# Weight sums in buffers of their own, and activation factors split one stage earlier

## The chip, the core and the metric

The kernel runs on one core of one Trainium2 chip. The metric is the device time of one execution in microseconds. The core has a matrix engine (TensorE, PE in the profile; PEld is its weight load), a vector engine (VectorE, DVE), a scalar engine (ScalarE, ACT), GpSimd (POOL) and SyncE (SP), which here only issues DMAs. Each engine takes its instructions in the order in which they stand in its queue: one that waits holds up all behind it.

## What is computed

One residual layer over 512 tokens of width 2048, then the final norm:

```python
h = rmsnorm(x, norm1_g)
u = h @ cc_w_in + cc_b_in
val, gate = jnp.split(u, 2, axis=-1)
u = causal_dwconv(val * jax.nn.sigmoid(gate), cc_dw) + cc_dw_b
x = x + (jax.nn.silu(layernorm(u, cc_ln_g, cc_ln_b)) @ cc_w_out + cc_b_out)
h2 = rmsnorm(x, norm2_g)
x = x + jnp.square(jax.nn.relu(h2 @ mlp_w1)) @ mlp_w2
out = rmsnorm(x, final_g)
```

`mlp_w1` is 2048 x 8192, `mlp_w2` is 8192 x 2048. All is float32.

## The kernel before

Every float32 matrix product is made of three products of a shorter type, fp32r: each factor is rounded to a high part (`wh`, `ah`) and the rest is its low part (`wl`, `al`), and `mm3` (L277) adds high x high, high x low and low x high. The profile shows them as L280, L281 and L282.

The first half of the program is the convolution layer. This case is about the MLP behind it, in two stages.

**The first product** (L790 to L840) runs over 64 tiles f of 128 hidden units. For each, two chunks of weights are loaded, split (`Plain.make`, L121: high part on ACT, low part on DVE or POOL) and multiplied with the 16 tiles of h2. DVE takes the result out with relu and a scale (L823), ACT squares it (L824). Two f make a pair n. The result of a pair is a 2 x 2 block matrix of 256 tokens by 128 hidden units: a11, a12, a21, a22, and POOL makes four sums of it (s1 to s4, L832 to L835). Seven left factors of 256 columns, a11, a22, a12 and the four sums, are written to DRAM (`spill[n]`) by DMAs that ACT issues, one for the three blocks and one for the four sums.

**The second product** uses a scheme of seven products for a 2 x 2 block product: P1 to P7, each of one left factor (sum of activation blocks) and one right factor (a block or difference of blocks of `mlp_w2`). It runs over 8 groups g of four pairs. A group has two passes q (the two halves of the output columns); a pass (`seven`, L848) has 14 chunks, the seven products for each half hs of the group, in the order ORDER. I write P5,1 for product P5 of half 1. A chunk is 12 matmuls with one pair of `wh` and `wl`: two pairs i of the half, two halves of 128 tokens, three matmuls each. In the last group, only half 0 is done this way, and the last two pairs are multiplied plainly (`last_pair`, L896).

The right factors are made by `Factor.make` (L151). `Sums.get` (L135) loads the four blocks b11, b12, b21, b22 of a half, in one buffer each. POOL makes the differences, each written over one of its own inputs: P5 = b12 - b11 into b11 (L162), P6 into b11 (L165), P7 into b12 (L168), P4 into b11 (L171). ACT rounds the factor to `wh` (L172), ACT copies `wh` to the matrix engine's accumulators (`ax`, L178) and DVE subtracts (L179, two halves of a chunk); for P2 alone POOL subtracts (L174).

**Buffers.** The ring of `wh` has four buffers, so has that of `wl`: a chunk's high part is made when the chunk four before has been used. Blocks b12 and b22 lie in the four "raw" buffers that also carry the plain weights, b11 and b21 in five "rb" buffers, which in the first product hold `four` and `sums`.

**Activation factors.** `fetch(n)` (L774) loads the seven factors of a pair as they are into one of two buffers `seven`, by a DMA of SP; `prepare(n)` (L779) rounds and subtracts them on ACT (L786) and DVE (L787) into `ah` and `al` of one of seven slots. The tables FETCH and PREP say behind which chunk (q, step) of a group this is put for the four pairs of the next group. A slot is free when the pair seven before has been used.

Outside the stretches marked as scheduled by hand, a scheduler sets the order of each engine's instructions when the program is built.

Of the kernel before, what the change touches and what calls it, by code (L numbers as in the profile page):

```python
# [57 lines left out]
BLOCKS = ("11", "12", "21", "22")  # L58
# [21 lines left out]
HT = T // 2  # L80
# [3 lines left out]
def trunk(ctx: ExitStack, tc: tile.TileContext, xT, vec, fg, w_in, w_out, w1, w2s, w2b, out):  # L84
    nc = tc.nc
# [7 lines left out]
    wts = ctx.enter_context(tc.tile_pool(name="wts", bufs=4))  # L93
# [7 lines left out]
    dram = ctx.enter_context(tc.tile_pool(name="dram", bufs=1, space=bass.MemoryType.DRAM))  # L101
# [26 lines left out]
    class Sums:  # L128


        def __init__(self, src):
            self.src = src
            self.raw = {}

        def get(self, b, hs):  # L135
            if (b, hs) not in self.raw:
                pool, tag, n = (wts, "raw", 4) if b[1] == "2" else (mlp[0], "rb", 5)
                t = pool.tile([P, 1024], F32, tag=tag, name=f"b{b}", bufs=n)
                nc.sync.dma_start(out=t, in_=self.src[BLOCKS.index(b), hs])
                self.raw[b, hs] = t  # L140
            return self.raw[b, hs]

    class Factor:
# [5 lines left out]
                self.sums.get(b, self.hs)  # L149

        def make(self, hi, lo):  # L151
            b11, b12, b21, b22 = (self.sums.raw.get((b, self.hs)) for b in BLOCKS)
            sub = ALU.subtract
            if self.product == "P1":
                s = b11
            elif self.product == "P2":
                s = b21
            elif self.product == "P3":
                s = b22
            elif self.product == "P5":  # L160
                s = b11
                nc.gpsimd.tensor_tensor(out=s, in0=b12, in1=b11, op=sub)  # L162
            elif self.product == "P6":
                s = b11
                nc.gpsimd.tensor_tensor(out=s, in0=b22, in1=b11, op=sub)  # L165
            elif self.product == "P7":
                s = b12
                nc.gpsimd.tensor_tensor(out=s, in0=b22, in1=b12, op=sub)  # L168
# [3 lines left out]
            nc.scalar.copy(out=hi, in_=s)  # L172
            if self.product in LO_POOL:
                nc.gpsimd.tensor_tensor(out=lo, in0=s, in1=hi.bitcast(F32), op=sub)  # L174
                return
            for sl in (slice(0, 512), slice(512, 1024)):
                st = bank("ax")
                nc.scalar.copy(out=st, in_=hi[:, sl].bitcast(F32))  # L178
                nc.vector.tensor_tensor(out=lo[:, sl], in0=s[:, sl], in1=st, op=sub)  # L179
# [585 lines left out]

    NPAIR = FF // P // 2
    LASTS = NPAIR - GROUP // 4
    spill = [dram.tile([P, 7 * HT], F32, name=f"spill{n}") for n in range(NPAIR)]
    acc = []
    row2 = None  # L770
    pairs = {}
    raws = {}

    def fetch(n):  # L774
        raws[n] = mlp[0].tile([P, 7 * HT], F32, tag="seven", name="seven", bufs=2)
        width = 7 * HT if n < LASTS else 4 * HT
        nc.sync.dma_start(out=raws[n][:, :width], in_=spill[n][:, :width])

    def prepare(n):  # L779

        seven = raws.pop(n)
        i = n % SLOTS
        hi = slots[i].tile([P, 7 * HT], F32R, tag=f"ah{i}", name="ah", bufs=1)
        lo = slots[i].tile([P, 7 * HT], F32R, tag=f"al{i}", name="al", bufs=1)
        for sl in (slice(0, 3 * HT), slice(3 * HT, 7 * HT)):
            nc.scalar.copy(out=hi[:, sl], in_=seven[:, sl])  # L786
            nc.vector.tensor_tensor(out=lo[:, sl], in0=seven[:, sl], in1=hi[:, sl].bitcast(F32), op=ALU.subtract)  # L787
        pairs[n] = (hi, lo)

    for f in range(FF // P):  # L790
        ps = bank()
        for c in range(2):
            wh, wl = chunk()
            for i in range(8):
                k = 8 * c + i
                sl = slice(i * P, (i + 1) * P)
                mm3(ps, (wh[:, sl], wl[:, sl]), h2[k], k == 0, k == NT - 1)
        if row2 is None:
            st = bank("ax")
            col_sums(st, acc1)  # L800
# [24 lines left out]
        if n >= LASTS:
            nc.scalar.dma_start(out=spill[n][:, f % 2 * T :][:, :T], in_=here)
        elif f % 2:
            a21, a11, a22, a12 = (four[:, i * HT : (i + 1) * HT] for i in range(4))
            sums = mlp[0].tile([P, 4 * HT], F32, tag="rb", name="sums", bufs=5)
# [5 lines left out]
            nc.gpsimd.tensor_tensor(out=s4, in0=a12, in1=s2, op=ALU.subtract)  # L835
            nc.scalar.dma_start(out=spill[n][:, 3 * HT :], in_=sums)
        if f >= FF // P - 8 and f % 2 == 0 and f < FF // P - 2:
            fetch((f - (FF // P - 8)) // 2)
        elif f >= FF // P - 8 and f % 2 and f < FF // P - 2:
            prepare((f - (FF // P - 7)) // 2)  # L840
# [4 lines left out]
    prepare(3)  # L845


    def seven(g, q, halves):  # L848
# [20 lines left out]
        for step, (product, hs) in enumerate(ORDER):  # L869
# [36 lines left out]

    for q in range(2):
# [18 lines left out]
    for b in range(NTOK):  # L926
# [6 lines left out]
        for i, cs in enumerate(pieces):  # L933
# [9 lines left out]
            sq = mlp[0].tile([P, 1024], F32, tag="rb", name="sq", bufs=5)  # L943
# [61 lines left out]
```

## Time and profile before

| | us |
|---|---|
| three runs | 1999.8, 1999.65, 1997.3 (median 1999.65) |
| profiled execution, device time | 1997.83 |
| its span, first to last instruction | 1996.0 |
| mean granted TensorE clock over the span | 0.987 |
| first product, about | 600 to 1288 |
| second product | 1288 to 1945 |
| norm and output behind it | 1945 to 1996 |

The page divides the span into 40 slices; slices 13 to 25 are the first product, 26 to 39 the second. "idle before us <-releaser" in a row of the profile is the time the engine stood still ahead of such an instruction, and who ended the wait.

```profile
PE   6999999989999999999999999998989889898998
DVE  8999999971142311111111111377676766777675
ACT  5443444462343322222222222377676666776662
POOL 5799899746642433333333333465455565555563
```

In the first product (1 to 4 tenths on DVE, ACT and POOL) the other engines have much room; in the second DVE and ACT are at 6 to 7 tenths, and PE has slices of 8.

### The profile page before, as it was taken

To read this page: it belongs to the slowest core of one execution; us is meant where nothing else is said; L and a number is where in the kernel's file an instruction comes from. 1 tells how busy PE (TensorE), PEld (TensorE's weight loads), DVE (VectorE), ACT (ScalarE), POOL (GpSimd) and SP (SyncE) were. 2 spreads that over 40 slices of the span, in tenths; PEclk is the share of its full clock that TensorE was granted. 3 is DMA by queue.
4 is the path that set the end of the run, shared out by engine and by line. 5 is a ranking of instruction groups with operands and counts; after the bars stand their busy time and mean duration, and the time that the engine had idled before them with its cause. 6 is when DMAs were issued, how large, how long until landed. Compare 5 with 4: busy or idle time off the path is not lost.

```text
span 1996.0 us, 23068 instructions
## 1 busy us (share of the span) xinstructions
PE 1908.2 (96%) x8578; PEld 1567.2 (79%) x8578; DVE 1082.8 (54%) x1512; ACT 923.3 (46%) x1286; POOL 1084.5 (54%) x625
## 2 busy tenths in 40 slices
PE   6999999989999999999999999998989889898998
PEld 4888888988888888888888888877777777777776
DVE  8999999971142311111111111377676766777675
ACT  5443444462343322222222222377676666776662
POOL 5799899746642433333333333465455565555563
PEclk9999999999999999999999999999999999999999
DMA  5222332133234444334343433344443433343323
GB/s 215 87 85 95 107 136 95 33 127 121 91 106 144 174 158 150 134 132 150 132 141 138 147 132 137 133 165 132 164 148 127 158 118 125 121 157 131 116 85 106
DMA packets 73552, 257.15 MB, mean 129 GB/s; under 512 B 8160, under 2 KB 8800, under 8 KB 73440
## 3 DMA queue, kind: packets, MB, share of 16 engines
q1 hardware_dynamic: 63792, 225.99, 33.5%
q10 hardware_dynamic: 9648, 29.69, 3.7%
q8 instruction: 67, 1.10, 0.2%
q14 instruction: 45, 0.37, 0.1%
HBM read 222.88 MB, written 32.77 MB: 128 GB/s over the span
## 4 chain that ended last, share of the span: by engine, by line
PE 58%; DVE 14%; issue 12%; POOL 10%; DMA 3%; ACT 1%; SPq 0%; POOLq 0%; DVEq 0%; ACTq 0%
PE mm L281 17%; PE mm L282 16%; PE mm L280 16%; PE mm L651 8%; DVE ax L356 4%; POOL b L162 4%; POOL b L168 3%; DMA b<-in_w2s 3%; DVE wl L179 2%; DVE x L866 2%; POOL wl L174 2%; POOL b L171 1%; DVE al L787 1%; POOL b L165 1%; DVE xl L274 1%
## 5 line engine op out<-in xcount | busy, mean ns | idle before, releaser
L126 POOL TENSOR_TENSOR wl<-raw,wh 128x1024 fp32r<-128x1024 f32 x151 | 365.3, 2430 | 508.6 <-ACT wh L125 505.8
L125 ACT CAST wh<-raw 128x1024 fp32r<-128x1024 f32 (+1 forms) x221 | 230.1, 1048 | 631.4 <-PE mm L281 399.0
L281 PE MATMUL mm<-yl,wh 128*128 128x512 f32 x1024 | 398.7, 389 | 0.2 <-DVE yl L274 0.2
L280 PE MATMUL mm<-yh,wh 128*128 128x512 f32 x1024 | 398.7, 389 | 0.0
L282 PE MATMUL mm<-yh,wl 128*128 128x512 f32 x1024 | 398.6, 389 | 0.0
L281 PE MATMUL mm<-wl,ah 128*128 128x512 f32 x840 | 339.3, 404 | 36.7 <-DVE wl L179 24.9
L280 PE MATMUL mm<-wh,ah 128*128 128x512 f32 x840 | 331.2, 397 | 16.2 <-ACT wh L172 14.3
L282 PE MATMUL mm<-wh,al 128*128 128x512 f32 x840 | 332.9, 397 | 0.0
L179 DVE TENSOR_TENSOR wl<-b,ax 128x512 fp32r<-128x512 f32 x360 | 231.5, 681 | 169.0 <-ACT ax L178 92.6
L172 ACT CAST wh<-b 128x1024 fp32r<-128x1024 f32 x210 | 217.2, 1050 | 191.9 <-POOL b L162 127.1
L126 DVE TENSOR_TENSOR wl<-raw,wh 128x1024 fp32r<-128x1024 f32 (+1 forms) x70 | 89.5, 1279 | 353.8 <-ACT wh L125 353.8
L281 PEld LDWEIGHTS mm<-wl,ah 128*128 128x128 f32 x840 | 161.5, 192 | 87.7 <-DVE wl L179 35.4
L281 PEld LDWEIGHTS mm<-yl,wh 128*128 128x128 f32 x1024 | 192.2, 188 | 40.3 <-DVE yl L274 0.6
L280 PEld LDWEIGHTS mm<-yh,wh 128*128 128x128 f32 x1024 | 192.2, 188 | 39.8
L282 PEld LDWEIGHTS mm<-yh,wl 128*128 128x128 f32 x1024 | 192.2, 188 | 39.7
L356 DVE SCALAR_TENSOR_TENSOR ax<-u,v,ax 128x512 f32<-128x512 f32 x327 | 218.2, 751 | 0.0
L280 PE MATMUL mm<-xh,wh 128*128 128x512 f32 (+1 forms) x544 | 206.4, 379 | 5.5 <-ACT wh L125 5.4
L282 PE MATMUL mm<-xh,wl 128*128 128x512 f32 (+1 forms) x544 | 205.9, 379 | 4.0 <-DVE wl L126 4.0
L281 PE MATMUL mm<-xl,wh 128*128 128x512 f32 (+1 forms) x544 | 206.9, 380 | 2.5 <-DVE xl L274 2.4
L178 ACT COPY ax<-wh 128x512 f32<-128x512 f32 x360 | 200.6, 585 | 17.7 <-DVE wl L179 15.1
L280 PEld LDWEIGHTS mm<-wh,ah 128*128 128x128 f32 x840 | 160.5, 192 | 55.9 <-ACT wh L172 17.8
L162 POOL TENSOR_TENSOR b<-b,b 128x1024 f32<-128x1024 f32 x30 | 77.2, 2574 | 222.6 <-DVE wl L179 209.8
(172 smaller groups left out, 2577.5 us busy)
## 6 DMA issues: line engine op xcount, KB each, us to landing
raw<-in_w SPq DMA_DIRECT2D x128, 512.0 KB, 3.3
b<-in_w2s SPq DMA_DIRECT2D x120, 512.0 KB, 4.3
raw<-in_w_in SPq DMA_DIRECT2D x63, 512.0 KB, 3.3
seven<-spill SPq DMA_DIRECT2D x30, 896.0 KB, 4.7
raw<-in_w_out SPq DMA_DIRECT2D x32, 512.0 KB, 3.3
spill<-sums ACTq DMA_DIRECT2D x30, 512.0 KB, 2.6
spill<-four ACTq DMA_DIRECT2D x30, 384.0 KB, 2.3
xt<-in_xT SPq DMA_DIRECT2D x16, 256.0 KB, 5.8
```

The source lines that it names most:

```text
L125: nc.scalar.copy(out=hi[:, sl], in_=raw[:, sl])
L126: (nc.vector if sl.stop == cut else self.eng).tensor_tensor(out=lo[:, sl], in0=raw[:, sl], in1=hi[:, sl].bitcast(F32), op=ALU.subtract)
L162: nc.gpsimd.tensor_tensor(out=s, in0=b12, in1=b11, op=sub)
L168: nc.gpsimd.tensor_tensor(out=s, in0=b22, in1=b12, op=sub)
L172: nc.scalar.copy(out=hi, in_=s)
L178: nc.scalar.copy(out=st, in_=hi[:, sl].bitcast(F32))
L179: nc.vector.tensor_tensor(out=lo[:, sl], in0=s[:, sl], in1=st, op=sub)
L280: nc.tensor.matmul(out=ps, lhsT=wh, rhs=xh, start=first, stop=False, **how)
L281: nc.tensor.matmul(out=ps, lhsT=wh, rhs=xl, start=False, stop=False, **how)
L282: nc.tensor.matmul(out=ps, lhsT=wl, rhs=xh, start=False, stop=last, **how)
L356: nc.vector.scalar_tensor_tensor(out=o, in0=a, scalar=w, in1=c, op0=ALU.mult, op1=ALU.add)
L651: nc.tensor.matmul(out=ps[n][:, sl], lhsT=a[:, wsl], rhs=x[:, sl], start=first and a is wh and x is hi, stop=last and x is lo)
```

## The change

- P5's difference gets a buffer of its own, b5, in the "raw" ring, next to b22. P6 = b22 - b5 is written over b11, P7 over b12 as before, P4 = b21 - b11 over b21. So b11, b12 and b21 lie in "rb", which has eight buffers instead of five: twelve buffers for ten blocks and differences of a pass instead of nine for eight. Blocks are asked for three items ahead instead of two.
- The activation factors are rounded and split in the first product's stage (`split`), and both parts are written to DRAM: four DMAs per pair instead of two, with twice the bytes. The DMA of a low part is issued behind the next tile's square (the list `later`). `prepare`, its instructions in the second product and the buffers `seven` are gone.
- `fetch` loads high and low part straight into the slot, by two DMAs of GpSimd; FETCH has new places, and the first three pairs are fetched behind tiles 8, 10 and 12 of the first product. `last_pair` fetches in the same way.

```diff
-PREP = ((0, 3), (0, 9), (1, 2), (1, 12))
-FETCH = ((0, 0), (0, 4), (0, 10), (1, 3))
+FETCH = ((0, 2), (0, 6), (0, 10), (1, 12))
...
+        def buffer(self, b):
+
+            pool, tag, n = (wts, "raw", 4) if b in ("22", "5") else (mlp[0], "rb", 8)
+            return pool.tile([P, 1024], F32, tag=tag, name=f"b{b}", bufs=n)
...
             elif self.product == "P5":
-                s = b11
-                nc.gpsimd.tensor_tensor(out=s, in0=b12, in1=b11, op=sub)
+                raw["5", hs] = self.sums.buffer("5")
+                s = less("5", "12", "11")
             elif self.product == "P6":
-                s = b11
-                nc.gpsimd.tensor_tensor(out=s, in0=b22, in1=b11, op=sub)
+                s = less("11", "22", "5")
...
-        LOAD = 2
+        LOAD = 3
...
+    def split(n, x, sl):
+
+        width = sl.stop - sl.start
+        hi = mlp[0].tile([P, 4 * HT], F32R, tag="rb", name="ah", bufs=8)
+        lo = mlp[0].tile([P, 4 * HT], F32R, tag="rb", name="al", bufs=8)
+        nc.scalar.copy(out=hi[:, :width], in_=x)
+        nc.scalar.dma_start(out=spill[n][:, 0, sl], in_=hi[:, :width].bitcast(F32))
+        nc.vector.tensor_tensor(out=lo[:, :width], in0=x, in1=hi[:, :width].bitcast(F32), op=ALU.subtract)
+        later.append((spill[n][:, 1, sl], lo[:, :width].bitcast(F32)))
...
+        pairs[n] = tuple(slots[i].tile([P, 7 * HT], F32R, tag=f"{x}{i}", name=x, bufs=1) for x in ("ah", "al"))
+        for y in range(2):
+            nc.gpsimd.dma_start(out=pairs[n][y], in_=spill[n][:, y, :])
...
-            nc.scalar.dma_start(out=spill[n][:, : 3 * HT], in_=four[:, HT:])
...
-            nc.scalar.dma_start(out=spill[n][:, 3 * HT :], in_=sums)
...
+            split(n, four[:, HT:], slice(0, 3 * HT))
+            split(n, sums, slice(3 * HT, 7 * HT))
+        if f in (8, 10, 12):
+            fetch((f - 8) // 2)
```

**POOL in a q=1 pass.** Before, the whole work of the fourth pass (blocks b11_10417 and so on of half 0, b11_10498 of half 1) stood in one piece:

```order
L162 TENSOR_TENSOR b11_10417<-b12_10441,b11_10417 128x1024
L168 TENSOR_TENSOR b12_10441<-b22_10567,b12_10441 128x1024
L165 TENSOR_TENSOR b11_10417<-b22_10567,b11_10417 128x1024
L174 TENSOR_TENSOR wl_10527<-b21_10473,wh_10526 128x1024
L162 TENSOR_TENSOR b11_10498<-b12_10524,b11_10498 128x1024
L168 TENSOR_TENSOR b12_10524<-b22_10593,b12_10524 128x1024
L174 TENSOR_TENSOR wl_10596<-b21_10542,wh_10595 128x1024
L165 TENSOR_TENSOR b11_10498<-b22_10593,b11_10498 128x1024
L171 TENSOR_TENSOR b11_10417<-b21_10473,b11_10417 128x1024
L171 TENSOR_TENSOR b11_10498<-b21_10542,b11_10498 128x1024
```

In the changed kernel the same pass reads so (L158 makes the differences, L179 the low part of P2; b5_10792 and b5_10862 are P5's of this pass, b5_11122 is that of the pass behind it):

```order
L158 TENSOR_TENSOR b5_10792<-b12_10711,b11_10685 128x1024
L158 TENSOR_TENSOR b12_10711<-b22_10833,b12_10711 128x1024
L158 TENSOR_TENSOR b5_10862<-b12_10788,b11_10761 128x1024
L158 TENSOR_TENSOR b12_10788<-b22_10858,b12_10788 128x1024
L158 TENSOR_TENSOR b11_10685<-b22_10833,b5_10792 128x1024
L158 TENSOR_TENSOR b5_11122<-b12_11045,b11_11019 128x1024
L179 TENSOR_TENSOR wl_10818<-b21_10735,wh_10817 128x1024
L158 TENSOR_TENSOR b21_10735<-b21_10735,b11_10685 128x1024
L158 TENSOR_TENSOR b11_10761<-b22_10858,b5_10862 128x1024
L179 TENSOR_TENSOR wl_10886<-b21_10815,wh_10885 128x1024
```

Five differences, and one of the pass behind, have moved ahead of P2's low parts.

**The fetches of a q=0 pass.** Before, ACT had the rounding of fetched pairs (L786) among the fifth pass's weight factors, the first of them waiting for the slot that pair 4 of the group before leaves:

```order
L786 CAST ah_10878<-seven_10659 128x768
L172 CAST wh_10862<-b21_10811 128x1024
L786 CAST ah_10878<-seven_10659 128x1024
L786 CAST ah_10997<-seven_10935 128x768
L172 CAST wh_10886<-b11_10834 128x1024
L786 CAST ah_10997<-seven_10935 128x1024
```

In the changed kernel POOL has the DMAs of the fetch (L794) among that pass's work; the first waits for PE, which reads the slot to the end of P4,0 of the pass before:

```order
L158 TENSOR_TENSOR b11_11019<-b22_11167,b5_11122 128x1024
L794 DMA ah_11163<-spill11_5032 128x1792
L179 TENSOR_TENSOR wl_11148<-b21_11069,wh_11147 128x1024
L794 DMA al_11164<-spill11_5032 128x1792
L794 DMA ah_11261<-spill12_5033 128x1792
L794 DMA al_11262<-spill12_5033 128x1792
L179 TENSOR_TENSOR wl_11220<-b21_11145,wh_11219 128x1024
L158 TENSOR_TENSOR b11_11095<-b22_11192,b5_11196 128x1024
L794 DMA ah_11357<-spill13_5034 128x1792
L794 DMA al_11358<-spill13_5034 128x1792
```

The fetches have moved from SP to POOL, ahead of and between the low parts of P2,0 and P2,1, and the rounding is gone from ACT.

**ACT in the first product.** Before, behind the second square of a pair (L824), two DMAs and then the next weights' rounding:

```order
L824 ACTIVATE four_7806<-four_7806 128x512
L831 DMA spill19_5040<-four_7806 128x768
L836 DMA spill19_5040<-sums_7872 128x1024
L125 CAST wh_7880<-raw_7882 128x1024
L125 CAST wh_7910<-raw_7912 128x1024
```

In the changed kernel, two roundings and three DMAs stand there, and a fourth behind the next weights':

```order
L830 ACTIVATE four_7574<-four_7574 128x512
L784 CAST ah_7647<-four_7574 128x768
L785 DMA spill16_5037<-ah_7647 128x768
L784 CAST ah_7652<-sums_7642 128x1024
L832 DMA spill16_5037<-al_7648 128x768
L785 DMA spill16_5037<-ah_7652 128x1024
L124 CAST wh_7658<-raw_7660 128x1024
L832 DMA spill16_5037<-al_7653 128x1024
```

The next weights' rounding has moved behind both activation roundings and the wait for the first low part.

More of the change, by code (lines that the diff above doesn't have):

```diff
@@ L133, in __init__ @@
             self.raw = {}
+        def buffer(self, b):
+            pool, tag, n = (wts, "raw", 4) if b in ("22", "5") else (mlp[0], "rb", 8)
+            return pool.tile([P, 1024], F32, tag=tag, name=f"b{b}", bufs=n)
         def get(self, b, hs):
             if (b, hs) not in self.raw:
[L137 to L138 removed]
+                self.raw[b, hs] = t = self.buffer(b)
                 nc.sync.dma_start(out=t, in_=self.src[BLOCKS.index(b), hs])
[L140 removed]
             return self.raw[b, hs]
@@ L767, in trunk @@
     LASTS = NPAIR - GROUP // 4
-    spill = [dram.tile([P, 7 * HT], F32, name=f"spill{n}") for n in range(NPAIR)]
+    spill = [dram.tile([P, 2, 7 * HT], F32, name=f"spill{n}") for n in range(NPAIR)]
     acc = []
@@ L771, in trunk @@
     pairs = {}
-    raws = {}
-    def fetch(n):
[L775 to L781, printed above, removed]
-        i = n % SLOTS
[L783 to L788, printed above, removed]
+    later = []
+    def split(n, x, sl):
[6 more added lines that the diff above has]
+        later.append((spill[n][:, 1, sl], lo[:, :width].bitcast(F32)))
+    def fetch(n):
+        i = n % SLOTS
+        pairs[n] = tuple(slots[i].tile([P, 7 * HT], F32R, tag=f"{x}{i}", name=x, bufs=1) for x in ("ah", "al"))
+        for y in range(2):
+            nc.gpsimd.dma_start(out=pairs[n][y], in_=spill[n][:, y, :])
     for f in range(FF // P):
@@ L820, in trunk @@
         if f % 2 == 0:
-            four = mlp[0].tile([P, 4 * HT], F32, tag="rb", name="four", bufs=5)
+            four = mlp[0].tile([P, 4 * HT], F32, tag="rb", name="four", bufs=8)
         here = four[:, f % 2 * T :][:, :T]
@@ L824, in trunk @@
         nc.scalar.activation(out=here, in_=here, func=AF.Square)
+        for x in later:
+            nc.scalar.dma_start(out=x[0], in_=x[1])
+        later = []
         if n >= LASTS:
-            nc.scalar.dma_start(out=spill[n][:, f % 2 * T :][:, :T], in_=here)
+            split(n, here, slice(f % 2 * T, f % 2 * T + T))
         elif f % 2:
             a21, a11, a22, a12 = (four[:, i * HT : (i + 1) * HT] for i in range(4))
-            sums = mlp[0].tile([P, 4 * HT], F32, tag="rb", name="sums", bufs=5)
+            sums = mlp[0].tile([P, 4 * HT], F32, tag="rb", name="sums", bufs=8)
             s3, s1, s2, s4 = (sums[:, i * HT : (i + 1) * HT] for i in range(4))
-            nc.scalar.dma_start(out=spill[n][:, : 3 * HT], in_=four[:, HT:])
             nc.gpsimd.tensor_tensor(out=s3, in0=a11, in1=a21, op=ALU.subtract)
@@ L835, in trunk @@
             nc.gpsimd.tensor_tensor(out=s4, in0=a12, in1=s2, op=ALU.subtract)
-            nc.scalar.dma_start(out=spill[n][:, 3 * HT :], in_=sums)
[L837 to L840, printed above, removed]
+            split(n, four[:, HT:], slice(0, 3 * HT))
+            split(n, sums, slice(3 * HT, 7 * HT))
+        if f in (8, 10, 12):
+            fetch((f - 8) // 2)
+    for x in later:
+        nc.scalar.dma_start(out=x[0], in_=x[1])
     left.close()
@@ L844, in trunk @@
     fetch(3)
-    prepare(3)
     def seven(g, q, halves):
@@ L896, in last_pair @@
     def last_pair(n):
-        fetch(n)
-        four = raws.pop(n)
         for f in range(2):
-            here = four[:, f * T : (f + 1) * T]
             both = [lasts[0].tile([P, T], F32R, name="ah", tag=f"ah{len(a)}"),
-                    lasts[0].tile([P, T], F32R, name="al", tag=f"al{len(a)}") if len(a) < 3 else mlp[0].tile([P, T], F32R, tag="rb", name="al", bufs=5)]
-            nc.scalar.copy(out=both[0], in_=here)
-            nc.vector.tensor_tensor(out=both[1], in0=here, in1=both[0].bitcast(F32), op=ALU.subtract)
+                    lasts[0].tile([P, T], F32R, name="al", tag=f"al{len(a)}") if len(a) < 3 else mlp[0].tile([P, T], F32R, tag="rb", name="al", bufs=8)]
+            for y in range(2):
+                nc.gpsimd.dma_start(out=both[y], in_=spill[n][:, y, f * T : (f + 1) * T])
             a.append(both)
```

21 lines of the change are left out of this document (10 added, 11 removed).

## Prediction

> **What bounds the kernel now.** I read the page's first part, then stretches of the span by engine, then the timeline of the worst stretch.
>
> ```profile
> span 1996.0 us, 23068 instructions
> PE 1908.2 (96%) x8578; PEld 1567.2 (79%) x8578; DVE 1082.8 (54%) x1512; ACT 923.3 (46%) x1286; POOL 1084.5 (54%) x625
> ```
>
> No engine but PE is near full. Whether PE is at its pace is told by matmuls per microsecond, not by busy time (columns: stretch, length, then busy us and count of PE, PEld, DVE, ACT, POOL, granted clock, DMA share, GB/s):
>
> ```profile
> 612.00:1280.00 668.00, 668.00 (x2948) 553.13 (x2948) 128.85 (x132) 171.10 (x195) 239.08 (x182) 1.00 0.42 149
> 1287.98:1369.35 81.37, 77.90 (x337) 62.52 (x336) 62.86 (x83) 60.65 (x85) 46.32 (x18) 1.00 0.46 159
> 1369.35:1457.22 87.87, 79.80 (x337) 63.51 (x336) 61.92 (x86) 60.37 (x85) 50.17 (x20) 0.98 0.40 138
> 1810.04:1898.25 88.21, 81.20 (x338) 64.50 (x336) 61.72 (x88) 60.78 (x87) 50.17 (x20) 0.96 0.34 112
> 1898.25:1940.50 42.25, 38.12 (x156) 29.88 (x155) 33.17 (x53) 29.03 (x44) 26.80 (x14) 0.96 0.24 75
> 1545.08:1592.32 47.24, 41.92 (x170) 32.87 (x168) 37.47 (x46) 32.42 (x45) 25.38 (x10) 0.93 0.47 167
> 1592.32:1633.10 40.78, 38.85 (x169) 31.31 (x168) 24.58 (x40) 27.95 (x41) 24.80 (x11) 1.00 0.32 103
> ```
>
> The first product is at pace: 668.00/2948 = 0.2266 us per matmul. In the second a group (two passes, 336 matmuls) would be 76.1 us at that pace. The first group takes 81.37 (5.2 lost), the six between 1369.35 and 1898.25 take 528.90 together (the first and last are shown; 72.1 lost), and the 156 matmuls after them 42.25 for 35.3 (6.9 lost). **In all 84.2 us are lost in the second product**, and a q=0 pass (47.24 for 38.1) loses three times what a q=1 pass does (40.78). Where one group loses them:
>
> ```profile
> 1552.24 0.50 PE L281 MATMUL mm<-wl,ah 128*128 128x512 f32 x1 [1.33 <-POOL wl L174]
> 1558.69 1.11 PE L280 MATMUL mm<-wh,ah 128*128 128x512 f32 x2 [2.30 <-ACT wh L172]
> 1560.90 0.79 PE L281 MATMUL mm<-wl,ah 128*128 128x512 f32 x1 [1.10 <-DVE wl L179]
> 1561.91 0.63 PE L281 MATMUL mm<-wl,ah 128*128 128x512 f32 x1
> 1562.34 0.63 PE L282 MATMUL mm<-wh,al 128*128 128x512 f32 x1
> 1587.20 0.50 PE L281 MATMUL mm<-wl,ah 128*128 128x512 f32 x1 [0.59 <-DVE wl L179]
> 1598.81 0.50 PE L281 MATMUL mm<-wl,ah 128*128 128x512 f32 x1 [0.66 <-POOL wl L174]
> 1604.46 0.50 PE L281 MATMUL mm<-wl,ah 128*128 128x512 f32 x1 [1.26 <-DVE wl L179]
> ```
>
> PE waits for weight factors, three times early in a q=0 pass (after which matmuls follow at 0.43 us for about 3 us), once at its end, and twice in a q=1 pass. Who makes them late:
>
> ```profile
> 1540.20 2.40 POOL L162 TENSOR_TENSOR b<-b,b 128x1024 f32<-128x1024 f32 x1 [13.65 <-DVE wl L179]
> 1554.27 3.28 POOL L162 TENSOR_TENSOR b<-b,b 128x1024 f32<-128x1024 f32 x1 [2.09 <-DVE wl L179]
> 1588.42 2.40 POOL L162 TENSOR_TENSOR b<-b,b 128x1024 f32<-128x1024 f32 x1 [14.95 <-DVE wl L179]
> 1590.90 2.41 POOL L168 TENSOR_TENSOR b<-b,b 128x1024 f32<-128x1024 f32 x1
> 1596.38 2.37 POOL L174 TENSOR_TENSOR wl<-b,wh 128x1024 fp32r<-128x1024 f32 x1
> 1598.72 2.39 POOL L162 TENSOR_TENSOR b<-b,b 128x1024 f32<-128x1024 f32 x1
> ACT wh L172 <- POOL b L162: 127.1, 30, 6.5
> ```
>
> POOL stands idle 13 to 15 us before each pass, because L162 (P5) writes over b11, which P1's low part still reads. Then it works without a gap, a chunk behind PE's need: the L174 that ends at 1598.75 frees PE at 1598.81, the L162 after it leads through ACT and DVE to 1604.46. That is order, not load: POOL is busy 50.2 of 88 us.
>
> **The change, part by part.** *P5 in its own buffer.* The wait of 13.65 and 14.95 goes; P5's sum needs only its loads and a free "raw" buffer. What is late next? I walk the new order (PE's order at a pass boundary stays), with zero at the end of P7,1 of a pass. A chunk of 12 matmuls is 2.72 us. The ring of four wh buffers frees P2,0's high part at 4.1 (P4,0 ends) and P2,1's at 10.9; PE wants P2,0's low part at 11.1, P2,1's at 16.5.
>
> ```profile
> L172 ACT CAST wh<-b 128x1024 fp32r<-128x1024 f32 x210 | 217.2, 1050 | 191.9 <-POOL b L162 127.1
> L178 ACT COPY ax<-wh 128x512 f32<-128x512 f32 x360 | 200.6, 585 | 17.7 <-DVE wl L179 15.1
> L179 DVE TENSOR_TENSOR wl<-b,ax 128x512 fp32r<-128x512 f32 x360 | 231.5, 681 | 169.0 <-ACT ax L178 92.6
> ```
>
> A factor made by ACT and DVE needs 1.05 + 0.59 + 0.68 = 2.3 us from a free ring buffer to its first half, against leads of 5.4 to 8.2: no wait. In a q=1 pass POOL's row for the following pass's P5 waits for this pass's b5 to come free (P6's sum, and P5's low part, about 3.2); then five rows of 2.4 end P2,1's low part at 15.3, **1.2 us before PE wants it**. Thin, but a gain over 1.26 late.
>
> *GpSimd's fetches.* In a q=0 pass POOL stops until P4,0 ends (4.1), since pair 4g's slot is read until then. Behind that stand both low parts of P2. With d for one DMA on POOL, P2,0's is ready at 4.1 + max(d, 1.05) + 2.4, in time up to d = 4.6; P2,1's, behind four DMAs, at 9.0 + 4d (4.1, four times d, two low parts of 2.4), though not before 14.4, since its high part ends at 12.0; it is in time **up to d = 1.9**. No DMA runs on POOL in this trace; the nearest rows:
>
> ```profile
> 1574.63 0.33 SPq L777 DMA_DIRECT2D seven<-spill  x1
> seven<-spill SPq DMA_DIRECT2D x30, 896.0 KB, 4.7
> ```
>
> So d lies between 0.33 (an issue by SP) and 4.7 (POOL held until the same size has landed). At 0.33 nothing is late; at 4.7, P2,1 is 11.3 us late in seven groups, 79 us, and the gain is gone. I take 1, nearer to the issue, which waits for no data. The Trainium skill ("DMA: Bandwidth & Descriptors", Latency and other measured facts) gives about 1 us to the first byte for GpSimd's path, against 0.6 on the hardware path; by that P2,1 would be ready at 14.4 and the sum stands.
>
> [...] The POOL row at 1554.27 took 3.28 instead of 2.40, beside an L787 of DVE that reads two SBUF tiles. [...]
>
> *Activation factors.* Out of the second product go 30 x (2.01 + 1.85) = 115.7 us of DVE and 30 x (1.05 + 0.83) = 56.3 of ACT:
>
> ```profile
> L787 DVE TENSOR_TENSOR al<-seven,ah 128x1024 fp32r<-128x1024 f32 x30 | 60.2, 2006 | 6.8 <-ACT ah L786 6.8
> L787 DVE TENSOR_TENSOR al<-seven,ah 128x768 fp32r<-128x768 f32 x30 | 55.5, 1851 | 12.9 <-ACT ah L786 12.9
> L786 ACT CAST ah<-seven 128x1024 fp32r<-128x1024 f32 x30 | 31.4, 1046 | 0.0
> L786 ACT CAST ah<-seven 128x768 fp32r<-128x768 f32 x30 | 24.9, 830 | 17.5 <-DMA seven<-spill 17.5
> ```
>
> They stand there in q=0 passes, where the 0.59 at 1587.20 is; it goes too. In the first product ACT (171 of 668 busy) and DVE (129) take them, with two more DMA issues of 0.33 on ACT per pair.
>
> ```profile
> 1005.07 1.05 ACT L125 CAST wh<-raw 128x1024 fp32r<-128x1024 f32 x1 [4.38 <-PE mm L281]
> 1011.37 1.05 ACT L125 CAST wh<-raw 128x1024 fp32r<-128x1024 f32 x1 [4.72 <-POOL sums L835]
> ```
>
> The cast behind the sums comes about 2.5 us later; the ring of four, at 5.4 us a chunk, gives three chunks (16 us). I take nothing; without that cover it would be 30 x 2.5 = 75. The second write stream is 0.9 MB per 21.8 us, 42 GB/s on 149.
>
> *Fetch traffic.* A group moves 16 x 0.52 + 8 x 0.92 = 15.7 MB in 76 us, 206 GB/s, twice as much activation data as now, in a burst behind P4,0. Pair 4g+3 is wanted first, at 18: its low half, issued at about 9 after 2.4 of POOL work and behind its high half, lands near 15 at 4.7 us each. Bounds: nothing, or one landing late, 4.7 x 7 = 33; I take nothing. At the change of stage fetch(3) waits for the first product's end and is wanted 12 us later; 2 x 4.7 and two issues make 11.4, so I allow 2.
>
> **Sum.** 84.2 recovered; left over: one smallest stall (0.9 with its ramp, row 1587.20) in each of seven groups, 6; the change of stage, 2; half of the last passes' 6.9, which also hold waits for x, 4. Net 84 - 12 = 72. The profiled execution took 1997.8 (span 1996.0), 1.8 below the median of the three runs: 1997.8 - 72 = **1926 us**. All recovered would be 1913.6.
>
> **The rivals.** *POOL's DMAs are dear* (d from 1.9 to 4.7): low parts late by 4d - 7.5 in seven groups, at d = 3 some 31, and if the pace drops to 0.43 behind each as at 1561.91, 3 more each: 54 less gained, 1980; at d = 2.4, without such a ramp, 15 less, 1941. For it: nothing here shows d. Against: issues on SP cost 0.33. Chance 0.13. *The new wait for b5's buffer* eats its 1.2 us, or a fetch lands late: q=1 passes keep their 2.6, or pairs cost 3 a group; about 20 less, 1946. Chance 0.10. *No change*: the sums do get ahead, but PE waits as long for the split fetch; d near 4.7, 1997. Chance 0.03. *Slower:* POOL is held by each DMA past the landing. Its 50.2 us of work per group plus 8d then exceeds 88 from **d = 4.7**; at 6, 98 per group, 10 x 7 more, 2068. For it only that the fetch changes the type on its way, which no DMA here does. Chance 0.06. The forecast keeps 0.68.
>
> **How the numbers follow.** Range 1911 to 1966: from all recovered (with a little for the tail) over the second rival and half of the first; beyond it lie some 0.15. Faster by over 0.2% (about what a measurement of this kernel tells from no change) 0.91, within 0.2% 0.03, slower 0.06.
>
> **What would show it.** Groups of 336 matmuls near 77 us and granted clock 1.00; no long wait of POOL for a low part of DVE's before P5; the wait before POOL's fetch ended by PE; q=0 passes as short as q=1. POOL rows apart by more than 1.9 us around one fetch, or PE waiting for P2's low part behind fetches, speak for the first rival. The first product at more than 0.227 us per matmul, or second-product waits for a DMA, would make me wrong.

## The result and the profile after

| | before | after |
|---|---|---|
| median of four runs, us | 1999.7 (1997.3 to 2002.8) | **1928.1** (1927.3 to 1929.8) |
| ratio, 95% interval | | 0.9642 (0.9626 to 0.9659) |
| profiled execution, device time | 1997.83 | 1929.75 |
| its span | 1996.0 | 1928.0 |

Busy times on the changed kernel's page:

```profile
PE 1885.7 (98%) x8578; PEld 1565.3 (81%) x8578; DVE 1073.4 (56%) x1512; ACT 934.8 (48%) x1286; POOL 1122.3 (58%) x693
```

The number of matmuls is the same, so is the busy time of DVE, ACT and POOL within 40 us: the change moved work and order. Stretches of the changed kernel (columns as before: stretch, length, busy us and count of PE, PEld, DVE, ACT, POOL, granted clock, DMA share, GB/s), the first product, then the first and the seventh group of the second and its last 159 matmuls:

```profile
612.00:1280.00 668.00, 668.00 (x2948) 553.12 (x2948) 214.51 (x186) 220.90 (x249) 269.87 (x192) 1.00 0.52 191
1290.90:1371.62 80.72, 76.80 (x338) 62.91 (x337) 48.58 (x76) 55.62 (x78) 48.28 (x29) 1.00 0.61 217
1756.93:1835.26 78.33, 76.47 (x338) 63.01 (x337) 48.14 (x76) 54.61 (x76) 54.66 (x34) 1.00 0.55 192
1835.26:1873.00 37.74, 36.52 (x159) 29.22 (x158) 36.23 (x53) 28.84 (x44) 20.57 (x11) 1.00 0.31 86
```

The first product is at the same pace as before (668.00 for 2948 matmuls), though DVE is busy for 214.51 us in it instead of 128.85 and ACT for 220.90 instead of 171.10. The first group takes 80.7 us instead of 81.4, the six behind it 76.4 to 78.3 instead of 88, and the granted clock is 1.00 in all of them. The two passes of the fourth group apart, 76.39 us together, the q=0 pass first:

```profile
1525.51:1563.59 38.08, 38.08 (x170) 31.54 (x168) 24.07 (x38) 27.30 (x38) 28.45 (x18) 1.00 0.80 298
1563.59:1601.90 38.31, 38.31 (x169) 31.46 (x168) 24.07 (x38) 27.30 (x38) 23.67 (x12) 1.00 0.35 115
```

The q=0 pass, which lost 9.1 us before, is at pace. Apart from 1.7 us in the last passes, what is lost yet lies in q=1 passes. PE's waits in two of them, of the second and of the seventh group:

```profile
1421.42 0.50 PE L286 MATMUL mm<-wl,ah 128*128 128x512 f32 x1 [0.45 <-POOL wl L179]
1808.14 0.50 PE L286 MATMUL mm<-wl,ah 128*128 128x512 f32 x1 [1.86 <-POOL wl L179]
```

### The profile page after: what moved, and what is told of

Its sections match the earlier page's. It is cut to its first block, busy times and chain, and to the rows that moved or that the text cites. A ratio compares the mean times of both kernels' runs of the same rounds, so it can differ in the third digit from the quotient of the medians.

```text
span 1928.0 us, 23365 instructions
## 1 busy us (share of the span) xinstructions
PE 1885.7 (98%) x8578; PEld 1565.3 (81%) x8578; DVE 1073.4 (56%) x1512; ACT 934.8 (48%) x1286; POOL 1122.3 (58%) x693
## 4 chain that ended last, share of the span: by engine, by line
PE 84%; DVE 8%; POOL 4%; issue 3%; ACT 1%; DMA 1%; DVEq 0%; SPq 0%; POOLq 0%; ACTq 0%
PE mm L286 25%; PE mm L287 25%; PE mm L285 25%; PE mm L656 8%; POOL b L158 2%; DVE ax L361 1%; POOL wl L179 1%; DVE wl L184 1%; DVE x L874 1%; DVE xl L279 1%; DVE dl L545 1%; PE ax L818 0%; DMA b<-in_w2s 0%; DVE d L623 0%; DVE wl L125 0%
## 5 line engine op out<-in xcount | busy, mean ns | idle before, releaser
L158 POOL TENSOR_TENSOR b<-b,b 128x1024 f32<-128x1024 f32 x120 | 288.7, 2417 | 148.7 <-DVE wl L184 83.5
L286 PE MATMUL mm<-wl,ah 128*128 128x512 f32 x840 | 327.7, 390 | 8.9 <-POOL wl L179 8.9
L285 PE MATMUL mm<-wh,ah 128*128 128x512 f32 x840 | 327.2, 390 | 1.2 <-DVE x L874 1.2
L287 PE MATMUL mm<-wh,al 128*128 128x512 f32 x840 | 326.7, 389 | 0.0
L874 DVE TENSOR_TENSOR x<-x,mm 128x512 f32<-128x512 f32 x224 | 149.6, 684 | 83.9 <-PE mm L287 83.9
```

Source lines behind the costliest of these rows:

```text
L158: nc.gpsimd.tensor_tensor(out=raw[to, hs], in0=raw[x, hs], in1=raw[y, hs], op=sub)
L285: nc.tensor.matmul(out=ps, lhsT=wh, rhs=xh, start=first, stop=False, **how)
L286: nc.tensor.matmul(out=ps, lhsT=wh, rhs=xl, start=False, stop=False, **how)
L287: nc.tensor.matmul(out=ps, lhsT=wl, rhs=xh, start=False, stop=last, **how)
L874: nc.vector.tensor_tensor(out=x2, in0=x2, in1=banks[x][s], op=ALU.add)
```

## The experiments

The prediction gave the 84.2 us of stalls almost wholly to POOL's order. So the first runs take the two halves of the change apart: P5's place, and the stage in which the activation factors are split.

**inplace: P5 over b11 again, the rest as changed.**

```diff
-                raw["5", hs] = self.sums.buffer("5")
-                s = less("5", "12", "11")
+                s = less("11", "12", "11")
...
-                s = less("11", "22", "5")
+                s = less("11", "22", "11")
...
-                s = less("21", "21", "11")
+                s = less("11", "21", "11")
```

> The changed kernel with one part undone: P5's difference is written over b11 again, and P6 and P4 over b11 too, as before; the split in the first product, GpSimd's fetches and the counts of buffers stay. Theory O (the gain came from POOL's order: P5 no longer waits for P1's low part): POOL's long waits of 11 to 15 us for a low part of DVE come back ahead of each pass, P2,0's low part and P5,1's factors are late in each, a pass loses between 2.6 us (the q=1 pass of the kernel before) and 9 us (its q=0 pass): a group 5 to 12 us over 76.1, the time 1960 to 2010. Theory L (the gain came from the 116 us of DVE and 56 us of ACT that left the second product; POOL's wait was only DVE being behind): POOL's wait shrinks to a few us, groups near 77, the time below 1940.

Measured: 1952.9, 24.8 over the changed kernel, between the ranges of the two theories. Two passes of this run, POOL ahead of them, and PE in the q=1 pass:

```profile
1530.47:1569.97 39.50, 38.96 (x170) 31.22 (x168) 23.61 (x38) 25.89 (x37) 27.09 (x18) 1.00 0.84 292
1569.97:1610.70 40.73, 38.87 (x169) 31.30 (x168) 24.57 (x40) 27.89 (x41) 24.76 (x12) 1.00 0.33 104
...
1525.58 4.89 POOL L158 TENSOR_TENSOR b<-b,b 128x1024 f32<-128x1024 f32 x2 [13.66 <-DVE wl L183]
...
1576.42 0.50 PE L285 MATMUL mm<-wl,ah 128*128 128x512 f32 x1 [0.62 <-POOL wl L178]
1582.07 0.50 PE L285 MATMUL mm<-wl,ah 128*128 128x512 f32 x1 [1.23 <-DVE wl L183]
```

POOL's wait of 13.66 us ahead of the q=0 pass is back, and so is the q=1 pass of the kernel before, wait for wait (0.62 and 1.23 here, 0.66 and 1.26 there; 40.73 us here, 40.78 there). But the q=0 pass takes 39.5 instead of 47.2, with that long wait of POOL ahead of it. P5's place makes the q=1 pass slow; it does not make the greater part of the q=0 pass's loss.

**splitlate: b5 stays, the activation factors are split in the second product again.**

```diff
-        hi = mlp[0].tile([P, 4 * HT], F32R, tag="rb", name="ah", bufs=8)
...
+        nc.scalar.dma_start(out=spill[n][:, 1, sl], in_=x)
...
-        for y in range(2):
-            nc.gpsimd.dma_start(out=pairs[n][y], in_=spill[n][:, y, :])
+        rest.append(n)
+        nc.gpsimd.dma_start(out=pairs[n][1].bitcast(F32), in_=spill[n][:, 1, :])
+
+    def prepare():
+        n = rest.pop(0)
+        hi, lo = pairs[n]
+        for sl in (slice(0, 3 * HT), slice(3 * HT, 7 * HT)):
+            nc.scalar.copy(out=hi[:, sl], in_=lo[:, sl].bitcast(F32))
+            nc.vector.tensor_tensor(out=lo[:, sl], in0=lo[:, sl].bitcast(F32), in1=hi[:, sl].bitcast(F32), op=ALU.subtract)
```

> The changed kernel with the other part undone: the activation factors are written to DRAM as they are, fetched by one GpSimd DMA per pair into the slot of the low part, and rounded and subtracted there by ACT and DVE in the second product, 60 instructions each, as before; b5 and the twelve buffers stay. Theory O: no long wait of POOL for DVE before P5; DVE's 2.0 us pieces fit into the lead of a factor (5.4 to 8.2 us against 2.3), so groups of 77 to 79 us and a time of 1925 to 1945. Theory L: DVE is at 6 to 7 tenths again, the stalls of the kernel before come back, groups near 88, 1985 to 2000.

Measured: 1969.5, 41.3 over the changed kernel, again between the two ranges (1925 to 1945, and 1985 to 2000). Two passes, then DVE, POOL and PE in the first of them:

```profile
1540.67:1586.03 45.36, 41.48 (x170) 33.44 (x168) 36.76 (x47) 33.29 (x46) 29.11 (x14) 0.92 0.48 171
1586.03:1624.35 38.32, 38.32 (x170) 31.46 (x168) 24.04 (x38) 27.42 (x38) 23.68 (x12) 1.00 0.38 113
...
1544.26 0.96 DVE L798 TENSOR_TENSOR al<-al,ah 128x768 fp32r<-128x768 f32 x1 [1.33 <-ACT ah L797]
1549.93 6.36 DVE L798 TENSOR_TENSOR al<-al,ah 128x768 fp32r<-128x768 f32 x2
...
1546.50 5.68 POOL L159 TENSOR_TENSOR b<-b,b 128x1024 f32<-128x1024 f32 x2 [2.39 <-DVE wl L185]
1552.15 3.06 POOL L180 TENSOR_TENSOR wl<-b,wh 128x1024 fp32r<-128x1024 f32 x1
...
1555.26 0.80 PE L287 MATMUL mm<-wl,ah 128*128 128x512 f32 x1 [3.32 <-POOL wl L180]
```

This is the mirror image of inplace: the q=1 pass is at pace, the q=0 pass, in which DVE's subtractions lie, takes 45.4. The rows show how. A subtraction of 768 columns takes 0.96 us at 1544.26; the two at 1549.93, one of 768 and one of 1024 columns, take 6.36 beside POOL, where 0.96 and 1.21 (the row at 1554.12 below) would make 2.2. Of POOL's rows there, two take 5.68 and one 3.06 instead of 2.4 each. DVE and POOL hold each other up, P2,1's low part is late, and PE waits 3.32 us for it. The trace of before has the same in its q=0 pass, DVE first, then POOL:

```profile
1547.52 2.42 DVE L787 TENSOR_TENSOR al<-seven,ah 128x1024 fp32r<-128x1024 f32 x1 [0.34 <-ACT ah L786]
1550.46 2.53 DVE L787 TENSOR_TENSOR al<-seven,ah 128x768 fp32r<-128x768 f32 x1
1552.92 1.27 DVE L179 TENSOR_TENSOR wl<-b,ax 128x512 fp32r<-128x512 f32 x2
1554.12 1.21 DVE L787 TENSOR_TENSOR al<-seven,ah 128x1024 fp32r<-128x1024 f32 x1
...
1548.81 3.38 POOL L174 TENSOR_TENSOR wl<-b,wh 128x1024 fp32r<-128x1024 f32 x1
```

Two held subtractions stand ahead of L179 (P1,1's low part), and POOL's P5 at 1554.27 waits 2.09 us for that: P5's place and the subtractions meet in one chain.

**neither: both undone, with the changed kernel's buffers, loads and GpSimd's fetch** (the edits of inplace on top of splitlate).

> Both parts undone at once (P5 over b11, split in the second product), with the changed kernel's twelve buffers, blocks asked for three items ahead and GpSimd's fetch, one DMA per pair. Theory A (what the two single steps lost adds up: P5's place costs the 2.6 us of a q=1 pass and 1.4 of a q=0 pass, the late split 7 us of a q=0 pass): passes of 46 to 48 and 40.7 us, time 1985 to 2000. Theory B (the buffers, the earlier loads or the freed SP queue carry a part of the gain by themselves): under 1980.

```profile
1548.07:1593.75 45.68, 40.69 (x170) 32.28 (x169) 34.22 (x46) 32.08 (x45) 26.34 (x14) 0.96 0.52 173
1593.75:1634.85 41.10, 38.84 (x170) 31.30 (x169) 24.56 (x40) 28.12 (x41) 25.79 (x12) 1.00 0.31 103
```

Measured: 1997.4, ratio to before 0.9991 (0.9980 to 1.0002), the same time, with passes of 45.7 and 41.1. Theory A holds: eight rb buffers, earlier loads and the freed SP queue bring next to nothing by themselves (this group takes 86.8 us instead of 88.0, and nothing of it is seen in the time). The four kernels make a square:

| | q=0 pass | q=1 pass | time | over the changed kernel |
|---|---|---|---|---|
| changed kernel | 38.1 | 38.3 | 1928.1 | |
| P5 over b11 (inplace) | 39.5 | 40.7 | 1952.9 | 24.8 |
| split late (splitlate) | 45.4 | 38.3 | 1969.5 | 41.3 |
| both (neither) | 45.7 | 41.1 | 1997.4 | 69.3 |

24.8 + 41.3 = 66.1 of the 69.3: the parts nearly add up (the intervals of the two single steps leave each some 6 us), and **the split is the greater**.

**ownsum: the kernel before with b5, six rb buffers and one buffer seven.**

```diff
+            pool, tag, n = (wts, "raw", 4) if b in ("22", "5") else (mlp[0], "rb", 6)
...
+                self.sums.raw["5", self.hs] = s = self.sums.buffer("5")
...
-        LOAD = 2
+        LOAD = 3
...
-        raws[n] = mlp[0].tile([P, 7 * HT], F32, tag="seven", name="seven", bufs=2)
+        raws[n] = mlp[0].tile([P, 7 * HT], F32, tag="seven", name="seven", bufs=1)
```

> The kernel before with b5 in the raw ring, P4's difference over b21, six rb buffers instead of five, blocks asked for three items ahead, and one buffer seven instead of two to make room; SP's fetch and the split in the second product stay as before. Theory O: P5 waits no longer for P1's low part; ten buffers for ten blocks may hold loads back by some us a pass: 1930 to 1960. Theory L: 1985 or more.

Measured: 1987.6, ratio 0.9935 (0.9895 to 0.9975): less than splitlate's gain, and in the range of theory L. A POOL row, and a line of SP's waits (total, times, longest):

```profile
1588.20 2.41 POOL L164 TENSOR_TENSOR b<-b,b 128x1024 f32<-128x1024 f32 x1 [8.70 <-DMA b<-in_w2s]
...
SPq L779 <- DVE al L789: 202.5, 27, 32.1
```

POOL waits for blocks. SP's fetch waits up to 32 us for the single buffer seven, and the blocks' loads stand behind it on SP. The one buffer, taken for want of room, spoils this run as a test of b5, so its time speaks for neither theory; splitlate is the clean one.

**What in the late split costs: nolow, pieces, psum, psum1.** All start from splitlate. nolow leaves DVE's subtraction out:

```diff
-            nc.vector.tensor_tensor(out=lo[:, sl], in0=lo[:, sl].bitcast(F32), in1=hi[:, sl].bitcast(F32), op=ALU.subtract)
```

> The kernel with the late split and P5's own buffer, but DVE's subtraction for the activation factors is left out in the second product (60 instructions; the low parts are then the unsplit factors); ACT's rounding stays. If DVE's instructions make the q=0 passes 45.4 us: they return to 38 to 39, time 1925 to 1940. If ACT's rounding or the landing of the fetch does it: they stay above 43, 1955 or more.

```profile
1522.43:1563.22 40.79, 38.99 (x170) 31.30 (x168) 24.55 (x39) 33.39 (x46) 26.91 (x14) 1.00 0.54 190
```

Measured: 1939.5, in the range for DVE's instructions, though the q=0 pass takes 40.8 and not 38 to 39. DVE's subtraction makes 30 of the 41 us; the 11 that stay (ACT's rounding, the later use of a fetch) were not taken apart.

pieces cuts the subtraction into 256 columns each:

```diff
+            for o in range(sl.start, sl.stop, 256):
+                z = slice(o, o + 256)
+                nc.vector.tensor_tensor(out=lo[:, z], in0=lo[:, z].bitcast(F32), in1=hi[:, z].bitcast(F32), op=ALU.subtract)
```

> The kernel with the late split and P5's own buffer, DVE's subtraction for the activation factors in seven pieces of 256 columns a pair instead of two of 768 and 1024. If it is the length of one DVE instruction (0.95 to 2 us) ahead of a weight's low part that hurts: q=0 passes of 39 to 42, time 1932 to 1950. If it is their sum, or the port: still 44 to 47, 1960 to 1980.

Measured: 2032.3, ratio 1.0166 (1.0137 to 1.0196), longer than before and outside both ranges. The line's durations (min/median/max in ns), then DVE and POOL side by side:

```profile
L800 DVE TENSOR_TENSOR al<-al,ah x210: 408/418/5389, 632.8 to 1883.2; 128x256 fp32r<-128x256 f32 x105
...
1571.44 13.16 DVE L800 TENSOR_TENSOR al<-al,ah 128x256 fp32r<-128x256 f32 x5
...
1571.61 5.04 POOL L159 TENSOR_TENSOR b<-b,b 128x1024 f32<-128x1024 f32 x2 [2.25 <-DVE wl L185]
```

A piece takes 0.41 us, but 48 of the 210 take over 2 us beside POOL, most of them 2.5 to 2.6, about one of POOL's rows (2.52 here). Every one of the 48 ends 0.28 or 0.29 us after a row of POOL does, less than its own 0.41: a held piece is not slowed by a share, it waits until POOL's row is done. So each piece can be caught anew, which is how I read that shorter pieces are worse. The Trainium skill ("SBUF — State Buffer", SBUF: two separate sides) says that a DVE instruction with two SBUF inputs and a GpSimd instruction that reads SBUF contend for one port pair: the one that starts first keeps it for its whole length, and the other waits. By that rule a 0.41 us piece can wait for a whole POOL instruction, and these rows agree. The six longest, 5.26 to 5.39 us, do not follow from it: in the profile they start some 0.3 us ahead of POOL's row, while POOL issues a DMA, and still wait for two rows. Why is open.

psum lets DVE read the high part from the accumulators (no second SBUF operand), after four copies by ACT per pair; psum1 does so with the first of these copies alone, which all four subtractions then read:

```diff
+        for o in range(0, 7 * HT, 512):
+            sl = slice(o, min(o + 512, 7 * HT))
+            st = bank("ax")[:, : sl.stop - o]
+            nc.scalar.copy(out=st, in_=hi[:, sl].bitcast(F32))
+            nc.vector.tensor_tensor(out=lo[:, sl], in0=lo[:, sl].bitcast(F32), in1=st, op=ALU.subtract)
```

> The kernel with the late split and P5's own buffer, but DVE's subtraction reads the high part from the matrix engine's accumulators, where ACT copies it first (four pieces of up to 512 columns a pair), so that it has one SBUF operand as L185 has. DVE's time per pair stays near 2.6 us, ACT's grows by 2.3. If DVE hinders POOL by reading two SBUF operands (POOL rows of 2.8 to 3.4 us instead of 2.4 beside it): POOL rows at 2.4, q=0 passes 38 to 41, time 1930 to 1950. If DVE's time ahead of the weights' low parts does it: they stay at 44 or more, 1960 to 1975.

> The kernel with the late split and P5's own buffer, DVE's subtraction reading the accumulators as in psum, but ACT copies only the first 512 columns of a pair there and all four pieces subtract these (the other three pieces' low parts are so taken from the wrong high part); ACT's load is then 0.6 us a pair over that of the late split instead of 2.3. DVE's time per pair stays near 2.5 us, without a second SBUF operand. If the hold-up between DVE and POOL (a piece of 256 columns took from 0.41 to 5.39 us, POOL's rows 2.5 instead of 2.4) makes most of what DVE's subtraction costs (30 us of 41): 1930 to 1948. If DVE's time ahead of weights' low parts, or the fetch's landing, makes it: 1955 to 1990.

Measured: 1988.7 and 1960.6. The group of psum's subtractions (busy us, mean ns of one), POOL's differences in splitlate and in psum1, then psum1's two passes and POOL ahead of the second:

```profile
L802 DVE TENSOR_TENSOR al<-al,ax 128x512 fp32r<-128x512 f32 x90 | 59.2, 684 | 50.1 <-ACT ax L801 49.2
...
L159 POOL TENSOR_TENSOR b<-b,b 128x1024 f32<-128x1024 f32 x120 | 303.3, 2537 | 203.8 <-DMA b<-in_w2s 146.6
L159 POOL TENSOR_TENSOR b<-b,b 128x1024 f32<-128x1024 f32 x120 | 288.6, 2418 | 204.6 <-DMA b<-in_w2s 183.3
...
1533.82:1574.25 40.43, 38.70 (x169) 31.32 (x168) 29.14 (x48) 34.29 (x48) 23.93 (x13) 1.00 0.55 192
1574.25:1616.43 42.18, 39.98 (x169) 32.63 (x168) 27.47 (x45) 28.47 (x41) 25.86 (x13) 0.96 0.34 104
...
1567.34 4.88 POOL L159 TENSOR_TENSOR b<-b,b 128x1024 f32<-128x1024 f32 x2 [13.19 <-DMA b<-in_w2s]
```

The rows are those of the hold-up theory: the instruction takes 0.68 us, as L185 does, POOL's differences take 2.42 in the mean instead of 2.54, and psum1's q=0 pass falls to 40.4, where nolow's is. Without the second SBUF operand DVE's 2.4 us per pair cost that pass nothing more. But both times miss the theory's ranges, and psum1's lies in that of its rival (1955 to 1990), since q=1 passes get slow in turn: 42.2 and 40.6 by turns in psum1, 43.9 to 44.0 in most of psum's. There P2,1's low part is late by POOL, which starts on the pass after a wait of 13.19 us for a block (in psum 13.55, and 3.38 more for DVE). Why the blocks come late there was not found. So the hold-up is shown for the rows and for the q=0 pass; that it is all of the 30 us is not.

**cut8: each fetch in eight DMAs**, for the first and last rivals.

```diff
+            for k in range(8):
+                sl = slice(k * 224, (k + 1) * 224)
+                nc.gpsimd.dma_start(out=pairs[n][y][:, sl], in_=spill[n][:, y, sl])
```

> The changed kernel with each fetch of a pair cut into eight column pieces (64 DMAs of GpSimd a group instead of 8, 112 KB each). If a DMA takes the 0.55 us of POOL that the changed kernel's rows show whatever its size, POOL's work in a group is 52 + 56 x 0.55 = 83 us, over the 76.1 of PE: POOL is the bound, each of seven groups 83 to 88 us, the time 1975 to 2010, and PE waits for low parts of P2. If the cost goes with the bytes (0.07 us a piece), groups stay at 77 and the time at 1925 to 1935.

```profile
1594.86:1642.12 47.26, 41.71 (x170) 33.12 (x168) 23.09 (x36) 23.95 (x34) 42.87 (x64) 0.93 0.86 208
1642.12:1694.86 52.74, 40.90 (x169) 32.48 (x168) 25.19 (x40) 30.28 (x42) 38.19 (x21) 0.94 0.36 113
...
1599.12 4.28 POOL L796 DMA_DIRECT2D al<-spill  x8
```

Measured: 2086.7, ratio 1.0441 (1.0405 to 1.0477). Eight DMAs of 112 KB hold POOL for 4.28 us, 0.54 each, and those of 896 KB in the changed kernel hold it for 0.53 to 0.58 (one for 0.72): the price goes by the DMA, not by its bytes. I had expected 1975 to 2010, with groups of 83 to 88 from the sum of POOL's work; that sum is 81.1 us here (42.87 + 38.19), but the group takes 100.0. POOL stands still for the other 19, so its sum of work is a bound and not the price; which of its waits make them was not followed further.

**fetchsp: the fetch on SP's queue.**

```diff
-            nc.gpsimd.dma_start(out=pairs[n][y], in_=spill[n][:, y, :])
+            nc.sync.dma_start(out=pairs[n][y].bitcast(F32), in_=spill[n][:, y, :])
```

> The changed kernel with the fetches of the split factors on SP's queue instead of GpSimd's; nothing else changed. POOL gains 4.4 us a group. If the wait for the slot (until P4,0 of the pass before ends) holds the loads of blocks behind it on SP's queue, POOL waits for blocks and PE for sums: 1935 to 1960. If not, 1922 to 1930, and GpSimd's part in the change is worth nothing.

```profile
SPq L794 <- PE mm L287: 41.5, 20, 5.1
...
1372.77:1448.93 76.16, 76.16 (x337) 63.08 (x336) 48.13 (x76) 54.54 (x76) 47.82 (x21) 1.00 0.58 207
1753.57:1834.76 81.19, 78.34 (x338) 64.09 (x337) 48.14 (x76) 54.52 (x76) 50.06 (x29) 0.98 0.53 183
...
1766.84 0.53 PE L286 MATMUL mm<-wl,ah 128*128 128x512 f32 x1 [2.00 <-POOL wl L179]
```

Measured: 1926.5, ratio 0.9645 (0.9630 to 0.9659), the changed kernel's. SP does wait for the slots, 41.5 us in all, and no more than 5.1 at once. In total, who issues the fetch is worth nothing, but two effects cancel in that. The second to the sixth group take 76.16 us, PE's pace, where the changed kernel has 76.4 to 77.8: with eight DMAs less a group, POOL's low parts of P2 are in time. The seventh group takes 81.19 instead of 78.33: POOL's own DMAs for `last_pair` stand there ahead of P2,1's low part, six between 1758.65 and 1764.40, and PE waits 2.00 us for it. That is the first rival of the prediction, in one pass.

**p2dve and p3pool: the low part that POOL makes.**

```diff
-LO_POOL = ("P2",)
+LO_POOL = ()
```

(in p3pool `("P3",)`.)

> The changed kernel with P2's low parts made as all others are (ACT copies to the accumulators, DVE subtracts) instead of by POOL. What the changed kernel still loses in the second product, about 13.7 us, lies for 11 at P2's low parts, which POOL makes behind four to five differences (theory Q: POOL's queue order in q=1 passes, as the second rival of the prediction has it): all 11 come back, 1914 to 1919. Rival: DVE (48 of 77 us a group, 54 then) or ACT (54.6, 59.3 then) is late in turn, or the wait for b5's buffer goes on holding POOL: 1924 or more.

> The changed kernel with POOL making P3's low parts instead of P2's: the same number of instructions on POOL, DVE and ACT, but at the ninth and tenth chunk of a pass, where no difference stands ahead of them that PE wants soon. Theory Q (the place in POOL's queue, not its load): 1914 to 1920. Rival (POOL's load, or b22 held longer in the ring it shares with b5): 1926 or more.

Measured: 1919.5 (ratio 0.9607, 0.9593 to 0.9622), 0.5 us over its range, and **1917.8** (0.9597, 0.9581 to 0.9613), within it; both are faster than the changed kernel. A group of p3pool:

```profile
1366.95:1443.11 76.16, 76.16 (x338) 63.06 (x337) 48.07 (x76) 55.48 (x77) 52.05 (x29) 1.00 0.59 208
```

All seven groups of both are at PE's pace, the first too. With P3, POOL has as much work as in the changed kernel (52.05 us), so another place in its queue is enough; fetchsp shows for five groups that less work on POOL is enough too. About 3 us are left in p3pool's last two passes (waits for x of 0.77, 0.60 and 0.99 with what follows them), and the second product has nothing else to give at this pace of PE.

## Why the prediction was right, and where it was wrong

**The sum** was right: 1926 against 1928.1. In the profiled runs, of the 84.2 us, 13.1 are still lost where I left 12, and the second product starts 2.9 later (1290.90 for 1287.98): 84.2 - 13.1 - 2.9 = 68.2, and the two times differ by 1997.83 - 1929.75 = 68.1. The 2.9 us are there before the MLP begins, in code that the change leaves alone, and the starts of other profiles lie between and beyond (1289.05 in p2dve, 1290.79 in p3pool, 1291.90 in fetchsp). The terms of the 12 are less right than their sum: 6 were left for the groups behind the first and 6.8 are lost there, 2 for the change of stage and 4.6 are, 4 for the last passes and 1.7 are. That they cancel is luck.

**"That is order, not load"** was the step that failed. The prediction gave the q=0 pass's three early stalls to P5's place and only the 0.59 at its end to the work that leaves. The square shows that P5's place makes the q=1 pass's 2.6 us and some 1.4 of a q=0 pass, the late split some 7 of a q=0 pass. The sum came out because both were undone at once, and in that respect too it was luck. Had the change been P5's buffer alone, the same argument would have forecast 1925 to 1945, as my expectation of splitlate still did, where it took 1969.5.

**The POOL row of 3.28 beside L787** stands in the prediction, and its sum has no term for such meetings. They were already a cost of the kernel before: L787's mean for 1024 columns was 2.01 us, and the row at 1554.12, with no POOL row beside it but the one it holds up, took 1.21.

**The new queue of POOL in a q=0 pass** was walked rightly. POOL from the end of a q=1 pass on:

```profile
1446.15 0.57 POOL L794 DMA_DIRECT2D ah<-spill  x1
1448.51 2.39 POOL L179 TENSOR_TENSOR wl<-b,wh 128x1024 fp32r<-128x1024 f32 x1 [1.78 <-ACT wh L177]
...
1455.47 2.40 POOL L179 TENSOR_TENSOR wl<-b,wh 128x1024 fp32r<-128x1024 f32 x1 [2.98 <-ACT wh L177]
```

P7,1 ends two chunks (5.44 us) ahead of the pass's start at 1448.52, at 1443.08. P2,0's low part is done 7.8 us after that (7.6 by the formula at the measured d), P2,1's 14.8 (14.4 at the earliest), and PE wants them at 11.1 and 16.5. The stop for the slot alone does not show: the first DMA starts at 1446.15, 3.1 us after that zero, right behind a difference, and no wait of POOL in this trace is ended by PE, though the prediction named that as a sign. d was taken as 1 and is 0.53 to 0.58 (once 0.72), so the bound of 1.9 is far, and the first rival fell; cut8, and fetchsp's seventh group, show that its mechanism is real.

**The new wait for b5's buffer**, the second rival, came true in part. POOL in a q=1 pass:

```profile
1402.03 9.75 POOL L158 TENSOR_TENSOR b<-b,b 128x1024 f32<-128x1024 f32 x4 [1.97 <-DVE wl L184]
1411.74 2.42 POOL L179 TENSOR_TENSOR wl<-b,wh 128x1024 fp32r<-128x1024 f32 x1
1414.24 4.76 POOL L158 TENSOR_TENSOR b<-b,b 128x1024 f32<-128x1024 f32 x2
1418.96 2.40 POOL L179 TENSOR_TENSOR wl<-b,wh 128x1024 fp32r<-128x1024 f32 x1
```

The first of the four differences at 1402.03 is P5,1, whose inputs come from DMAs: its wait of 1.97 for DVE can only be for the buffer it writes. From there POOL runs without a gap to 1421.36, PE wanted the last row at 1420.97, and so the 1.2 us of margin were used up. The six groups behind the first lose 6.8 us in such passes (0.3 to 2.2 each), not 20; I had left 6 for "one smallest stall". That this wait makes all of it is not shown: in the seventh group, which loses most, POOL stands still for 5.80 us ahead of its differences with no releaser in the profile. The change of stage took 4.6 instead of 2 (the first group's 80.72 for 76.1, with two waits of PE for P2's low parts in its q=1 pass), the last passes 1.7 instead of 4 (37.74 for 159 matmuls, 36.0 at pace).

**What was costed at nothing** was nothing: the first product's pace, and the fetches' traffic (the fetches land 5.7 and 8.0 us after their issue instead of the 4.7 taken, but PE waits for none; its waits in the second product are all for low parts of P2 and for x).

## What to carry to other kernels

Ask of each instruction that shows two lengths what ran beside it: a DVE row twice its shortest, next to a POOL row a third too long, is a cost of the present kernel, and can be the cause of a stall. When a change does two things, work out a sum for each alone; a right total proves neither. In an in-order queue the place of an instruction can matter as much as the load: POOL's P3 instead of P2 took the last 10 us at the same busy time.

## What the runs showed that I had not expected

- A GpSimd DMA holds POOL for about 0.55 us whether it moves 112 or 896 KB.
- A DVE subtraction of two SBUF operands (256 columns, 0.41 us) took up to 5.39 us beside POOL's rows, and with such pieces the kernel took 63 us more than with the whole subtractions of splitlate.
